# One list of items for each feed-forward, a last product by seven, and x turned in the first group

## Chip, cores and metric

The kernel runs on one core of a Trainium2 chip. The metric is the device time of one execution in microseconds (us); lower is better.

## The reference

One layer of a hybrid encoder block, 256 tokens of width 2048, fp32, with two SwiGLU feed-forwards of inner width 5632 around a mixer and a cross-attention:

```python
x = x + 0.5 * swiglu_ffn(rms_norm(x, ffn1_norm), ffn1_w_in, ffn1_w_out)   # FF1
h = rms_norm(x, mix_norm); p = h @ w_mix_in
...                                          # convolution module | spatial gating
x = x + y @ w_mix_out
x = x + memory_cross_attention(rms_norm(x, xattn_norm), rms_norm(mem, mem_norm), w_q, w_kv, w_o)
x = x + 0.5 * swiglu_ffn(rms_norm(x, ffn2_norm), ffn2_w_in, ffn2_w_out)   # FF2
return rms_norm(x, final_norm)

def swiglu_ffn(h, w_in, w_out):
    gate, up = jnp.split(h @ w_in, 2, axis=-1)
    return (jax.nn.silu(gate) * up) @ w_out
```

## The kernel before

**Products.** Each fp32 operand is split in two parts, hi (a rounding cast on ScalarE, ACT) and lo (the rest, a subtract on VectorE, DVE), and each product is three matmuls on TensorE (PE): hi·hi, hi·lo, lo·hi. A weight tile arrives as `raw` (128 partitions x 1024 columns, 512 KB, a DMA on SyncE's queue, SP), is cast and subtracted into an `hl` tile (hi and lo, 8 KB a partition), and is read by PE as the moving operand, 512 columns at a time; the activations are the stationary operand.

**Feed-forward.** The first product of each has 11 groups of 512 gate and 512 up columns, and each group has 16 k-tiles, taken as 8 pairs. `PATTERNS` says how each pair is multiplied: C is plain, 24 matmuls of 128x512; S is "by seven", with sums of blocks of weights and of activations as operands, 7 products and 21 matmuls. In the seven, DVE builds the sums of weights (L500, L501, L507, L514 of before), each of which then is cast and subtracted like a tile. The first group is plain. For the k-tiles in `SUMMED` the lo part comes from a GpSimd DMA that adds to the negated hi, not from DVE. At a group's end `give` makes silu(gate)·up (L550), transposes it on DVE (L553), and stores it to DRAM (`h_away`). The second product needs h again: `back` loads it in four DMAs of 128 KB into a tile called `z` or `h`, and `turn` splits it into hA, hB and hC, the stationary operands. Each of 11 groups has two turns.

FF1's last product runs in two blocks of 1024 columns with 44 pairs, 11 of them by seven (5 in the first block, 6 in the second). FF2's last product runs as four blocks of 512 columns, all plain (`gemm_n`, L215 to L217; the last block token half by token half, `by_token`, L1337 to L1339), with 128 small DVE transposes beside it, which turn x from its feature-major tile xT into x2, where the result is added. Behind it come the final rms, the scaling (`give` of FF2) and the output.

**Order.** Loads, casts and subtracts are each kept in the order in which they were written (`in_turn`); where these stand among other work, and where everything else stands, a scheduler decides at build time. Tiles are taken in rotation: three `hl` tiles of a pool, two in `ring`, `hl_l` twice, `hl_h`, and, in FF1, half of `more`; four `raw` tiles of a pool, `spare`'s parts and `raw_h`.

**Addresses.** Tiles have a start address within a partition. In the program built from before every tile that PE reads as a 512-wide moving operand starts at a multiple of 64 bytes, but hl_h: it starts 32 bytes past one (217056). hl_l, the tile below it, reaches to 216064 in its last 512 columns. Two pads, `to_64` and `to_64_too` (L1316), are 32 bytes each.

Of the kernel before, what the change touches and what calls it, by code (L numbers as in the profile page):

```python
# [11 lines left out]
F32 = mybir.dt.float32  # L12
# [24 lines left out]
PATTERNS = ("SCSCSCCC", "SCSCSCCC")  # L37

SUMMED = ((2, 7, 13), (2, 7, 13))
# [3 lines left out]
OUT_S = ((9, 11, 13, 15, 17), (9, 11, 13, 15, 17, 19))  # L43
OUT_STEPS = (
    [0, 1, 2, 3, 4, 5, 6, 7, 8, 10, 9, 12, 11, 14, 13, 16, 15, 18, 17, 19, 20, 21],
    [9, 0, 11, 1, 13, 2, 15, 3, 17, 4, 19, 5, 6, 7, 8, 10, 12, 14, 16, 18, 20, 21],
# [31 lines left out]
def layer(ctx: ExitStack, tc: tile.TileContext, a: dict):  # L78
# [184 lines left out]

    def square_into(acc, x, first):
# [90 lines left out]

    class FeedForward:
# [4 lines left out]


        def __init__(self, stack, tags, x_hl, gain, w_in, pattern, summed, w_out=None, pair=False):
            self.w_out, self.out_forms = w_out, None
            self.x_hl, self.gain, self.w_in, self.pattern = x_hl, gain, w_in, pattern
            self.tags, self.pattern_sums = tags, summed
            self.spairs = [p for p, c in enumerate(pattern) if c == "S"]
# [6 lines left out]
            self.places = [back[:, 0], back[:, 1], self.stage[1]]  # L374
            self.away = [dram.tile([4, 32, 4, 2 * P], F32, name=f"h_away{j}{int(pair)}") for j in range(NG)]
            self.low = ExitStack()
            low = self.low.enter_context(tc.tile_pool(name="low", bufs=1))
            more = [low.tile([P, 2, 1024], F32R, name=f"hl_l{i}") for i in range(2)]
# [3 lines left out]
            more.append(high.tile([P, 2, 1024], F32R, name="hl_h"))  # L382
            over = high.tile([P, 1024], F32, name="raw_h")
            ring = big.tile([P, 4, 2, 1024], F32R, name="ring", tag=tags[0])
            self.ring = [ring[:, i] for i in range(2)] + more
# [5 lines left out]
            self.x2 = spare[:, :4096].rearrange("p (t d) -> p t d", t=2)  # L391
            self.free = spare[:, 4096:]
            self.sums = spare[:, 4096:5120]
            self.raws = [spare[:, i * 1024:(i + 1) * 1024] for i in (5, 0, 1, 2, 3)]
            self.raw_at = 0

            self.raws_summed = [self.raws.pop()]
            self.u = [spare[:, 6144 + i * 512:6144 + (i + 1) * 512] for i in range(4)]
            self.at = 0
            self.next = self.pe = None  # L400
            self.hA = self.hB = self.hC = None
            if pair:
                self.hls.append(self.ring.pop())
                self.raws_summed.append(over)
            else:
                self.raws.append(over)

        def parts(self, raw, n=1024, last=False):

            i = self.at % (3 + len(self.ring))  # L410
            self.at += 1
            hl = whl.tile([P, 2, 1024], F32R, name="hl") if last or i < 3 else self.ring[i - 3]
            self.cast = in_turn("cast", nc.scalar.copy(out=hl[:, 0, :n], in_=raw[:, :n]))  # L413
            newest[0] = in_turn("sub", nc.vector.tensor_tensor(  # L414
                out=hl[:, 1, :n], in0=raw[:, :n], in1=hl[:, 0, :n].bitcast(F32), op=ALU.subtract
            ))
            return hl

        def raw(self, j, k):
            i = self.raw_at % (4 + len(self.raws))  # L420
            self.raw_at += 1
            raw = wraw.tile([P, 1024], F32, name="raw") if i < 4 else self.raws[i - 4]

            self.load = in_turn("load", nc.sync.dma_start(
                out=raw, in_=self.w_in[j, :, k] if j < NG else self.w_out[j - NG, :, k]
            ))
            return raw

        def buffer(self, at):
            return at % 2  # L430

        def following(self, at):
            same = [i for i in range(at + 1, len(self.sums_at)) if self.buffer(i) == self.buffer(at)]
            return same[0] if same else None

        def summed(self, at):

            if at >= len(self.sums_at):
                return
            j, k = self.sums_at[at]  # L440
            raw, hl = self.raws_summed[self.buffer(at)], self.hls[self.buffer(at)]
            nc.sync.dma_start(out=raw, in_=self.w_in[j, :, k])
            nc.scalar.activation(out=hl[:, 1], in_=raw, func=AF.Copy, scale=-1.0)
            nc.scalar.copy(out=hl[:, 0], in_=raw)
            nc.gpsimd.dma_start(out=hl[:, 1], in_=self.w_in[j, :, k], accum_op=ALU.add)

        def summed_then(self, at):

            with tc.issue_after(self.load.ins), tc.issue_after(self.cast.ins):
                self.summed(at)  # L450

        def sides(self, i):

            k = 2 * self.spairs[i]
            xg = self.u[2 * (i % 2)].rearrange("p (k t) -> p k t", k=2)
            f = self.u[2 * (i % 2) + 1].rearrange("p (f n) -> p f n", f=4)
            for q in range(2):
                nc.scalar.activation(out=xg[:, q], in_=xT[:, k + q], func=AF.Copy, scale=self.gain(k + q))
            a11, a21, a12, a22 = xg[:, 0, :P], xg[:, 0, P:], xg[:, 1, :P], xg[:, 1, P:]
            nc.vector.scalar_tensor_tensor(out=f[:, 0], in0=a21, scalar=-1.0, in1=a22, op0=ALU.mult, op1=ALU.subtract)  # L460
            nc.vector.scalar_tensor_tensor(
                out=f[:, 1], in0=f[:, 0], scalar=-1.0, in1=a11, op0=ALU.mult, op1=ALU.subtract
            )
            nc.vector.tensor_tensor(out=f[:, 2], in0=a11, in1=a21, op=ALU.subtract)
            nc.vector.tensor_tensor(out=f[:, 3], in0=a12, in1=f[:, 1], op=ALU.subtract)
            split(self.forms[i][:, :, 0], self.forms[i][:, :, 1], f)
# [9 lines left out]
        def tied(self):  # L476

            return nullcontext() if self.pe is None else tc.issue_after(self.pe.ins)

        def noted(self, done):  # L480
            if self.pe is not None:
                self.pe = done
# [942 lines left out]
```

## Time and profile before

| | |
|---|---|
| median of 3 runs | 2082.53 us (2080.94 to 2082.72) |
| profiled execution | 2083.68 us; span of its instructions 2081.9 us |
| granted TensorE clock | 0.998 of full speed |
| PE busy | 2062.0 us, 99% of the span |
| DVE busy | 1656.1 us, 80% |
| ACT busy | 1165.8 us, 56% |
| moved by DMA | 465.42 MB, 224 GB/s mean |

In the profile's rows a line number is a line of the program; `acc<-hl,x_hl` names what is written and what is read, the moving operand first. "128*128 128x512" is a stationary tile of 128x128 and a moving one of 512 columns. A matmul's row gives its time from start to end; matmuls overlap, so the interval between two starts is shorter. "[1.48 <-ACT hl_h L413]" is idle time and what ended it. `x4` stands for four instructions in one row.

### The profile page before, as it was taken

What the parts mean: (1) busy time and instruction counts of PE and PEld (TensorE: products, weight loads), DVE (VectorE), ACT (ScalarE), POOL (GpSimd) and SP (SyncE); (2) the same over time, 40 slices, a digit from 0 to 9 for tenths busy, and PEclk for the clock granted to TensorE, in tenths of its full rate; (3) what the DMA queues carried; (4) which work ended last, traced back from release to release, by engine and by line L of the source; (5) the groups of instructions that cost most, each with busy time, mean ns of one, the idle gap of its engine ahead of it and who ended that gap; (6) DMA issues with size and microseconds to landing.
All of it is one profiled execution on the core that took longest, in us unless ns stands there. A gap on an engine that the chain in (4) does not pass through costs nothing.

```text
span 2081.9 us, 26631 instructions
## 1 busy us (share of the span) xinstructions
PE 2062.0 (99%) x9577; PEld 1719.7 (83%) x9577; DVE 1656.1 (80%) x2358; ACT 1165.8 (56%) x1480; POOL 67.7 (3%) x83
## 2 busy tenths in 40 slices
PE   9999999999999999999999999999999999989998
PEld 7788888888888888888888899888888888868886
DVE  6988888878897689889877666778888888876754
ACT  7666666545555554444665455565665566544443
POOL 0000000000000000000000000000000000000000
PEclk9999999999999999999999999999999999999999
DMA  9889888868666676666656543687888888776664
GB/s 366 264 262 280 258 242 258 261 198 264 193 200 236 205 239 199 182 182 185 181 192 194 187 157 124 199 313 223 260 257 261 242 250 258 215 224 194 193 192 152
DMA packets 138372, 465.42 MB, mean 224 GB/s; under 512 B 15360, under 2 KB 27008, under 8 KB 137856
## 3 DMA queue, kind: packets, MB, share of 16 engines
q1 hardware_dynamic: 129024, 430.15, 63.1%
q0 software_dynamic: 8640, 32.51, 8.5%
q8 instruction: 75, 1.23, 0.2%
q10 hardware_dynamic: 576, 1.06, 0.1%
q14 instruction: 57, 0.47, 0.1%
HBM read 450.03 MB, written 13.63 MB: 223 GB/s over the span
## 4 chain that ended last, share of the span: by engine, by line
PE 94%; DMA 2%; DVE 2%; SPq 0%; ACT 0%; issue 0%; POOL 0%; DVEq 0%; ACTq 0%
PE acc L345 12%; PE acc L347 12%; PE acc L344 12%; PE acc L166 8%; PE acc L216 8%; PE acc L217 8%; PE acc L215 8%; PE acc L174 4%; PE acc L332 4%; PE acc L331 4%; PE acc L333 4%; PE aux L331 1%; PE aux L332 1%; PE aux L333 1%; DMA z<-h_away 1%; PE acc L1338 1%
## 5 line engine op out<-in xcount | busy, mean ns | idle before, releaser
L136 ACT CAST hl<-raw 128x1024 fp32r<-128x1024 f32 (+1 forms) x315 | 326.8, 1040 | 355.9 <-PE acc L217 189.1
L137 DVE TENSOR_TENSOR hl<-raw,hl 128x1024 fp32r<-128x1024 f32 (+1 forms) x315 | 380.7, 1210 | 160.9 <-ACT hl L136 159.1
L413 ACT CAST hl<-raw 128x1024 fp32r<-128x1024 f32 (+1 forms) x109 | 106.6, 993 | 71.3 <-DVE raw L514 44.2
L414 DVE TENSOR_TENSOR hl<-raw,hl 128x1024 fp32r<-128x1024 f32 (+1 forms) x109 | 124.7, 1151 | 18.7 <-ACT hl L413 18.3
L414 DVE TENSOR_TENSOR hl<-spare,hl 128x1024 fp32r<-128x1024 f32 (+1 forms) x94 | 106.8, 1151 | 16.0 <-ACT hl L413 15.9
L413 ACT CAST hl<-spare 128x1024 fp32r<-128x1024 f32 (+1 forms) x94 | 91.3, 993 | 48.2 <-DVE spare L514 36.0
L345 PE MATMUL acc<-hl,x_hl 128*128 128x512 f32 x304 | 111.3, 391 | 0.5 <-DVE hl L414 0.4
L344 PE MATMUL acc<-hl,x_hl 128*128 128x512 f32 x304 | 107.6, 391 | 0.0
L216 PE MATMUL acc<-hl,x_hl 128*128 128x512 f32 x256 | 100.5, 393 | 0.0
L216 PE MATMUL acc<-hl,m_hl 128*128 128x512 f32 x256 | 100.3, 392 | 0.0
L217 PE MATMUL acc<-hl,m_hl 128*128 128x512 f32 x256 | 100.2, 392 | 0.0
L217 PE MATMUL acc<-hl,x_hl 128*128 128x512 f32 x256 | 99.9, 390 | 0.0
L347 PE MATMUL acc<-hl,x_hl 128*128 128x512 f32 x304 | 94.8, 390 | 0.0
L215 PE MATMUL acc<-hl,x_hl 128*128 128x512 f32 x256 | 90.9, 393 | 0.0
L215 PE MATMUL acc<-hl,m_hl 128*128 128x512 f32 x256 | 90.9, 392 | 0.0
L413 ACT CAST hl_l<-spare 128x1024 fp32r<-128x1024 f32 (+1 forms) x60 | 58.6, 991 | 32.6 <-DVE spare L514 24.8
L414 DVE TENSOR_TENSOR hl_l<-spare,hl_l 128x1024 fp32r<-128x1024 f32 (+1 forms) x60 | 68.2, 1148 | 10.2 <-ACT hl_l L413 10.2
L413 ACT CAST ring<-spare 128x1024 fp32r<-128x1024 f32 (+1 forms) x55 | 53.2, 985 | 33.5 <-DVE spare L514 27.9
L345 PEld LDWEIGHTS acc<-hl,x_hl 128*128 128x128 f32 x304 | 57.0, 188 | 13.0 <-DVE hl L414 1.3
L593 DVE TENSOR_TENSOR spare<-spare,acc 128x512 f32<-128x512 f32 x80 | 51.0, 681 | 21.0 <-PE acc L347 20.9
L344 PEld LDWEIGHTS acc<-hl,x_hl 128*128 128x128 f32 x304 | 57.3, 189 | 12.0
L414 DVE TENSOR_TENSOR ring<-spare,ring 128x1024 fp32r<-128x1024 f32 (+1 forms) x55 | 62.3, 1140 | 6.1 <-ACT ring L413 5.8
(617 smaller groups left out, 5539.2 us busy)
## 6 DMA issues: line engine op xcount, KB each, us to landing
spare<-in_ffn_w_in SPq DMA_DIRECT2D x173, 512.0 KB, 6.9
raw<-in_ffn_w_in SPq DMA_DIRECT2D x149, 512.0 KB, 6.2
raw<-in_ffn_w_out SPq DMA_DIRECT2D x138, 512.0 KB, 4.4
raws_out<-in_ffn_w_out SPq DMA_DIRECT2D x33, 512.0 KB, 5.1
raw<-in_w_mix_vg SPq DMA_DIRECT2D x32, 512.0 KB, 4.6
raw<-in_w_k SPq DMA_DIRECT2D x32, 512.0 KB, 3.9
raw<-in_w_v SPq DMA_DIRECT2D x32, 512.0 KB, 4.4
raw<-in_w_mix_out SPq DMA_DIRECT2D x32, 512.0 KB, 4.5
```

The costliest lines, as they stand in the source:

```text
L136: nc.scalar.copy(out=hl[:, 0, :size], in_=raw[:, :size])
L137: newest[0] = nc.vector.tensor_tensor(out=hl[:, 1, :size], in0=raw[:, :size], in1=hl[:, 0, :size].bitcast(F32), op=ALU.subtract)
L166: done = nc.tensor.matmul(acc, lhsT=hi[:, k], rhs=xs[k], start=first and k == 0, stop=last and k == kk - 1, skip_group_check=True,)
L215: nc.tensor.matmul(acc[t], lhsT=x[:, 0, s], rhs=hi[:, k], start=k0 + k == 0, stop=False)
L216: nc.tensor.matmul(acc[t], lhsT=x[:, 0, s], rhs=lo[:, k], start=False, stop=False)
L217: nc.tensor.matmul(acc[t], lhsT=x[:, 1, s], rhs=hi[:, k], start=False, stop=k0 + k == nk - 1)
L331: nc.tensor.matmul(acc, lhsT=x[0], rhs=hi, start=first, stop=False)
L344: nc.tensor.matmul(acc[t][g], lhsT=x[:, 0, s], rhs=hi[:, cols[g]], start=(t, g) in first, stop=False)
L345: nc.tensor.matmul(acc[t][g], lhsT=x[:, 0, s], rhs=lo[:, cols[g]], start=False, stop=False)
L347: done = nc.tensor.matmul(acc[t][g], lhsT=x[:, 1, s], rhs=hi[:, cols[g]], start=False, stop=last)
L413: self.cast = in_turn("cast", nc.scalar.copy(out=hl[:, 0, :n], in_=raw[:, :n]))
L414: newest[0] = in_turn("sub", nc.vector.tensor_tensor(out=hl[:, 1, :n], in0=raw[:, :n], in1=hl[:, 0, :n].bitcast(F32), op=ALU.subtract))
```

## The change

1. A class `Line` runs each feed-forward as one list of items in the order of PE's products. An item has loads, a cast and a subtract (`produce`, `subtract`), the products (`use`) and further parts (`post`). The list takes places for `hl` and `raw` tiles as they come free, and at its end ties every engine's instructions in the order in which they were written. A subtract is written after the next item's cast.
2. FF2's last product takes FF1's form: two blocks of 1024 columns, 11 of 44 pairs by seven in both feed-forwards (5 and 6). Only its last four items go token half by token half.
3. FF2's x is turned in its first group: eight DVE transposes of 128x512 (`x_turn`) into the tiles h and z, two stores of 1 MB (`x_away`), and in the second block eight loads (`x_again`) and the final gains, 3 MB together. For that, the host lays out x's features in another order.
4. The turns of h stand at the last six items of group 10 (turns 0 to 5) and at the first sixteen of block 0 (6 to 21); each pair of turns issues the load of a later group's h.
5. Both feed-forwards now have the same `SUMMED` tiles, (7, 13) in group 1, and both use `more`. raw_h and the pad to_64_too are dropped.

The core of the diff:

```diff
-SUMMED = ((2, 7, 13), (2, 7, 13))
-OUT_S = ((9, 11, 13, 15, 17), (9, 11, 13, 15, 17, 19))
+SUMMED = tuple([()] + [(7, 13)] + [(2, 7, 13)] * 8 + [(2, 7)] for _ in range(2))
+OUT_S = ((9, 11, 13, 15, 17, 19), (9, 11, 13, 15, 17, 19))
...
+        def subtract(self):
+            item, self.ahead = self.ahead, None
+            if item.make is None:
+                n, hl = item.n, item.hl
+                nc.vector.tensor_tensor(
+                    out=hl[:, 1, :n], in0=item.raw[:, :n], in1=hl[:, 0, :n].bitcast(F32), op=ALU.subtract
+                )
+            for key in item.frees:
+                self.raws.append(item.held[key][1])
+            self.fetch()
...
+            for s, item in enumerate(self.items):
+                if self.ahead is item:
+                    self.subtract()
+                if item.use is not None:
+                    item.use(item.hl)
+                if item.place is not None:
+                    self.places.append(item.place)
+                self.used = s + 1
+                self.produce()
+                for part in item.post:
+                    part()
+            last = {}
+            for i in traced[begin:]:
+                if i.engine in last:
+                    tc.add_manual_dep(
                        i, last[i.engine].name,
                        mybir.DependencyInfo(mybir.DependencyClass.NoSync, mybir.DependencyReason.DATA),
                        reason="line",
                    )
+                last[i.engine] = i
...
-            high.tile([P, 248], F32, name="to_1024")
-            over = high.tile([P, 1024], F32, name="raw_h")
...
+            if j == NG - 1:
+                flat[1].post.append(lambda: (ff.back(0), ff.back(1)))
+                flat[4].post.append(lambda: ff.back(2))
+                for i, item in enumerate(flat[-6:]):
+                    item.post.insert(0, ff.turn(i))
...
-        acc_0 = gemm_n(a["ffn2_w_out"][0], h, per=0.55, between=turns, after=0)
+        parts, _, _ = ff.block(0, first_place, lambda o: None)
+        flat = [item for part in parts for item in part]
+        for i in range(6, 2 * NG):
+            flat[i - 6].post.append(ff.turn(i))
...
-        st.tile([P, 8], F32, name="to_64_too")
...
+        after = {k: [lambda k=k: x_turn(k - 1)] for k in range(1, 9)}
+        after[6].append(x_leaves(0))
+        after[10] = [x_leaves(1)]
```

Without `to_64_too` all that lies behind the pool of small tiles moves by 32 bytes. In the program built from after, the tiles `more`, `hl_s`, `hl_out`, `hl_l`, `hl_h`, `hC`, `k_hl`, `p_hl`, `q_hl`, `v_hl`, `o` and a few small ones start 32 bytes past a multiple of 64; ring, the pool's hl, x_hl and more_out stay on a multiple. Counted over the instructions, 2610 matmuls of 512 columns read a moving operand that starts so (357 before), 192 of 256 columns (none), 16 of 128 (none), and 866 a stationary one (none).

SP's queue at the start of FF1, before (`h<-in_x` and `z<-in_x` are the loads of x for the squares, `gx<-in_xT` those of the transposed x):

```order
L647 DMA raw<-in_ffn_w_in 128x512 x2
L424 DMA raw<-in_ffn_w_in 128x1024
L741 DMA gx<-in_xT 128x512
L424 DMA raw<-in_ffn_w_in 128x1024
L733 DMA h<-in_x 128x1024
L424 DMA raw<-in_ffn_w_in 128x1024
L741 DMA gx<-in_xT 128x512
L424 DMA spare<-in_ffn_w_in 128x1024
L733 DMA h<-in_x 128x1024
L424 DMA spare<-in_ffn_w_in 128x1024
```

And now:

```order
L910 DMA raw<-in_ffn_w_in 128x512 x2
L420 DMA raw<-in_ffn_w_in 128x1024
L920 DMA gx<-in_xT 128x512
L889 DMA h<-in_x 128x1024
L420 DMA raw<-in_ffn_w_in 128x1024 x2
L920 DMA gx<-in_xT 128x512
L889 DMA h<-in_x 128x1024
L420 DMA spare<-in_ffn_w_in 128x1024 x2
L920 DMA gx<-in_xT 128x512
```

The first load of x stood behind weight tiles 1 and 2 (tile 0 is the one in halves) and now stands behind tile 1 alone; the others have moved up in the same way.

DVE's queue at the end of FF1's first group, before (L550 is the gating, L553 the transpose, L414 a subtract, L500 to L514 the sums of weights for a seven):

```order
L414 TENSOR_TENSOR hl_l_134<-spare,hl_l_134 128x1024
L414 TENSOR_TENSOR hl_h<-spare,hl_h 128x1024
L500 TENSOR_TENSOR spare<-raw 128x512
L501 TENSOR_TENSOR spare<-raw 128x512
L507 TENSOR_TENSOR raw<-spare,raw 128x512
L550 SCALAR_TENSOR_TENSOR h<-acc,r_x_111,h 128x4x128 x2
L553 STREAM_TRANSPOSE h<-h 128x1024
L414 TENSOR_TENSOR hl_h<-spare,hl_h 128x1024
L414 TENSOR_TENSOR more<-raw,more 128x1024
L414 TENSOR_TENSOR hl<-raw,hl 128x1024
L500 TENSOR_TENSOR spare<-raw 128x512
L501 TENSOR_TENSOR spare<-spare,raw 128x512
```

And now (L714 the gating, L717 the transpose, L428 a subtract, L628 to L635 the sums; `hl_l_134` and `hl_l_135` are the two tiles hl_l):

```order
L632 TENSOR_TENSOR raw<-sums,raw 128x512
L428 TENSOR_TENSOR hl<-sums,hl 128x1024
L428 TENSOR_TENSOR hl<-raw,hl 128x1024
L635 TENSOR_TENSOR raw<-raw 128x512
L428 TENSOR_TENSOR hl<-raw,hl 128x1024
L428 TENSOR_TENSOR ring<-raw,ring 128x512
L428 TENSOR_TENSOR ring<-raw,ring 128x1024
L628 TENSOR_TENSOR sums<-spare 128x512
L629 TENSOR_TENSOR sums<-spare 128x512
L428 TENSOR_TENSOR hl_l_134<-raw,hl_l_134 128x1024
L714 SCALAR_TENSOR_TENSOR h<-acc,r_x_111,h 128x4x128 x2
L717 STREAM_TRANSPOSE h<-h 128x1024
```

The subtracts of the first pair by seven and of the plain pair behind it have moved ahead of the gating and the transpose.

SP's queue at the entry of FF2's last product, before (`h_away` numbers go by group, 11122 is group 2):

```order
L560 DMA h<-h_away_11122 32x4x256 x4
L133 DMA raw<-in_ffn_w_out 128x1024
L560 DMA z<-h_away_11123 32x4x256 x4
L560 DMA z<-h_away_11124 32x4x256 x4
L560 DMA h<-h_away_11125 32x4x256 x4
L560 DMA z<-h_away_11126 32x4x256 x2
L133 DMA raw<-in_ffn_w_out 128x1024
L560 DMA z<-h_away_11126 32x4x256 x2
L133 DMA raw<-in_ffn_w_out 128x1024
L560 DMA z<-h_away_11127 32x4x256 x3
L133 DMA raw<-in_ffn_w_out 128x1024
L560 DMA z<-h_away_11127 32x4x256
```

And now (`b_` numbers go by group, 11112 is group 0; the rows begin in group 10):

```order
L420 DMA raw<-in_ffn_w_in 128x1024 x4
L726 DMA z<-b_11112 32x4x256 x4
L726 DMA z<-b_11113 32x4x256 x4
L720 DMA b_11121<-h 128x1024
L726 DMA h<-b_11114 32x4x256 x4
L420 DMA raw<-in_ffn_w_out 128x1024 x4
L726 DMA z<-b_11115 32x4x256 x4
L420 DMA raws_out<-in_ffn_w_out 128x1024 x4
L420 DMA raw<-in_ffn_w_out 128x1024 x2
L726 DMA z<-b_11116 32x4x256 x4
L420 DMA raw<-in_ffn_w_out 128x1024
L726 DMA h<-b_11117 32x4x256 x4
```

h's first loads have moved ahead of the second product's first weights, of which now ten tiles are issued before the load of group 4's h.

More of the change, by code (lines that the diff above doesn't have):

```diff
@@ L400, in __init__ @@
-            self.next = self.pe = None
+            self.raws_summed = [raws.pop() for _ in range(2)]
+            self.sums_at = [(j, k) for j in range(1, NG) for k in sums[j]]
             self.hA = self.hB = self.hC = None
[L402 to L434, printed above, removed]
@@ L447, in summed_then @@
[L447 to L462, printed above, removed]
[L463 to L466 removed]
+            self.out_forms = None
@@ new lines, in banks, with begins, into @@
+        def banks(self, b, names):
+            for name in names:
+                b[name] = bank(pa if name in "67" else ps, "aux" if name in "67" else "acc")
+        def begins(self, b, name):
+            first = name not in b["begun"]
+            b["begun"].add(name)
+            return first
+        def into(self, b, name, x, hi, lo, last=False):
+            if name not in b:
+                self.banks(b, "5761" if name in "5761" else "2348")
+            three(b[name], x, hi, lo, self.begins(b, name), last)
@@ new lines, in second_sum, with third_sum, use, go @@
+            def second_sum():
+                nc.vector.tensor_tensor(out=one()[:, lo], in0=sums[:, lo], in1=two()[:, hi], op=ALU.add)
+            def third_sum():
+                nc.vector.tensor_tensor(out=one()[:, lo], in0=two()[:, lo], in1=one()[:, lo], op=ALU.subtract)
+            def use(*parts):
+                def go(w):
+                    for name, x, s in parts:
+                        self.into(b, name, x(), w[:, 0, s], w[:, 1, s], last and name in "5761")
+                return go
@@ new lines, in x_again, with next_turn @@
+        def x_again():
+            nonlocal xT
+            line.raws.extend(ff.fixed([ff.sums]))
+            xT = xt.tile([P, KD, T], F32, name="xT", tag="x")
+            for k in range(0, KD, 8):
+                nc.gpsimd.dma_start(out=xT[:, k:k + 8], in_=a["xT"][:, k:k + 8])
+            rest["x_hl"] = gained_tile("S2")
+        def next_turn():
+            rest["turns"].pop(0)()
+        last = items[ff.ends[NG - 1] - 1]
+        items[ff.ends[NG - 1] - 5].post.append(raws_out)
+        last.post.append(more_out)
@@ L847, in layer @@
+        line.run()
+        turns = turned(rest["o2"], 1)
         x_hl = rest["x_hl"]
-        finish()
         r_mt = rms_cols(sm, D, "r_mt")
@@ new lines, in layer, with quarters @@
+        after[9] = [x_sums]
+        items = ff.begin(
+            lambda k: None, after, (r_x, inverse_root_parts(r_x, lambda: x_tot[0][:, 0, 0:2], 1.0 / D, RMS_EPS))
+        )
+        items[14].post.append(lambda: given(ff))
+        groups(ff, items)
+        rest = {}
+        sums = st.tile([P, 2, 4], F32, name="sums")
+        most = [st.tile([P, 1], F32, name=f"f_most{t}") for t in range(2)]
+        def quarters(o):
+            return [o[:, t, g * G:(g + 1) * G] for g in range(2) for t in range(2)]
@@ L1354, in layer @@
-        give(1, 4)
+        items[ff.ends[NG - 1] - 5].post.append(raws_out)
+        items[ff.ends[NG - 1] - 1].post.append(more_out)
+        parts, _, _ = ff.block(0, first_place, lambda o: None)
+        flat = [item for part in parts for item in part]
+        for i in range(6, 2 * NG):
+            flat[i - 6].post.append(ff.turn(i))
+        flat[16].post.append(hl_out)
+        items += flat
+        ff.in_high[0].until = len(items) - 1
+        parts, b, _ = ff.block(1, second_place, None)
```

910 lines of the change are left out of this document (555 added, 355 removed).

## The prediction

> **What bounds the kernel now.** I read the page first (span, busy shares, clock), then the groups of TensorE (PE) by form, then PE's waits, then windows and timelines around the few places where PE stands still.
>
> ```profile
> span 2081.9 us, 26631 instructions
> PE 2062.0 (99%) x9577; PEld 1719.7 (83%) x9577; DVE 1656.1 (80%) x2358; ACT 1165.8 (56%) x1480; POOL 67.7 (3%) x83
> PEclk9999999999999999999999999999999999999999
> L215 PE MATMUL acc<-hl,hB 128*128 128x512 f32 x96 | 33.5, 389 | 0.0
> ```
>
> PE is busy for 99% of the span at full clock, so the time is the number of matmuls times their interval, plus the few stalls. The 389 ns of the last row is one matmul from start to end; they overlap. The interval has to be read from starts:
>
> ```profile
> 22.86 1.07 PE L344 MATMUL acc<-hl_l,x_hl 128*128 128x512 f32 x4
> ...
> 25.58 1.10 PE L344 MATMUL acc<-hl_h,x_hl 128*128 128x512 f32 x4
> ...
> 28.38 1.09 PE L344 MATMUL acc<-hl,x_hl 128*128 128x512 f32 x4
> ...
> 31.12 1.07 PE L344 MATMUL acc<-hl,x_hl 128*128 128x512 f32 x4
> L345 PE MATMUL acc<-ring,x_hl 128*128 128x512 f32 x168 | 62.5, 389 | 0.0
> L345 PE MATMUL acc<-hl_l,x_hl 128*128 128x512 f32 x156 | 58.6, 389 | 0.0
> L345 PE MATMUL acc<-hl_h,x_hl 128*128 128x512 f32 x96 | 37.1, 396 | 0.0
> L347 PE MATMUL acc<-hl_h,x_hl 128*128 128x512 f32 x96 | 31.0, 396 | 0.0
> ```
>
> These are four k-tiles of one plain item, twelve 128x512 matmuls each. Twelve on hl_l take 25.58 − 22.86 = 2.72 us, 226.7 ns each; twelve on hl_h take 28.38 − 25.58 = 2.80 us, 233.3 ns each. So hl_h costs 6.7 ns more for each matmul, and the groups say the same of the whole kernel: 396 ns against 389 wherever hl_h is the moving operand. hl_h is in before the only moving tile of this width that starts 32 bytes past a multiple of 64 (front part: addresses). 6.7 of 226.7 ns is 3.0%, as one 64-byte piece more would be on the 32 pieces of a 2048-byte row; that reading is mine, the 6.7 ns is the trace's.
>
> The stalls stand in PE's waits and in three windows (busy us, instruction count):
>
> ```profile
> PE acc L216 <- DVE hl L137: 3.4, 3, 2.1
> PE acc L215 <- ACT hl L136: 3.0, 1, 3.0
> PE acc L331 <- ACT hl_h L413: 1.5, 1, 1.5
> 45.00:60.00 15.00, 13.10 (x53) 9.18 (x52) 9.44 (x12) 6.03 (x8) 0.00 (x0) 1.00 0.81 276
> 450.00:490.00 40.00, 39.15 (x169) 31.07 (x168) 38.16 (x59) 27.99 (x40) 0.00 (x0) 1.00 0.91 273
> 1828.00:1864.00 36.00, 29.56 (x119) 22.96 (x118) 28.23 (x46) 16.35 (x22) 0.00 (x0) 0.95 0.70 219
> ```
>
> The second and third columns are the window and PE's busy time with its matmuls. At 226.7 ns each, the loss is 15.0 − 53 × 0.2267 = 3.0 us at the end of the first group of FF1, 40.0 − 169 × 0.2267 = 1.7 us at the entry of FF1's last product, and 36.0 − 119 × 0.2267 = 9.0 us at the entry of FF2's last product. The chain of waits says what that last one is:
>
> ```profile
> 1811.40 3.93 DMA z<-h_away
> 1815.41 6.14 DMA raw<-in_ffn_w_out
> 1821.58 7.04 DMA z<-h_away
> 1832.89 2.43 DMA z<-h_away
> 1848.37 5.35 DMA raw<-in_ffn_w_out
> ```
>
> h comes back from DRAM and the new weights come in on one SP queue, each held up by the other's buffers, with PE waiting for the split weights at the end.
>
> **The change, part by part.** The sum is against the profiled execution (2083.68 us; the median of the runs is 1.15 us below, and I subtract that at the end).
>
> *Eleven pairs by seven in FF2's last product.* By the order of both kernels PE issues 8394 matmuls of 128x512 instead of 8427: 11 pairs × 3 = 33 fewer, 33 × 0.2267 = −7.5 us, all on the path. The additions it needs (five of 128x512 a pair on DVE, one more subtract) are paid beside PE, as FF1's last product does already.
>
> *Entry of FF2's last product.* Now the first two turns' loads stand ahead of the last weights of group 10, six turns fall inside group 10, and ten weight tiles are ahead of the next wait for h (third order fence). I take the 9.0 us as gone: −9.0. If the queue holds up in another way, up to all of it stays; that is a rival.
>
> *End of the first group of FF1.* What PE waits for there is DVE:
>
> ```profile
> 50.00 0.75 DVE L550 SCALAR_TENSOR_TENSOR h<-acc,r_x,h 128x512 f32<-128x512 f32 x1 [6.86 <-ACT h L548]
> 51.72 1.25 DVE L553 STREAM_TRANSPOSE h<-h 128x1024 f32<-128x1024 f32 x1
> 52.89 1.18 DVE L414 TENSOR_TENSOR hl_h<-spare,hl_h 128x1024 fp32r<-128x1024 f32 x1
> 53.99 1.21 DVE L414 TENSOR_TENSOR more<-raw,more 128x1024 fp32r<-128x1024 f32 x1
> ```
>
> DVE idles 6.86 us, then does the gating and the transpose, and only then the subtracts of the first pair by seven. The new order puts the six subtracts of the first pair by seven and of the plain pair after it ahead of the gating (second order fence): they fall into the idle time. −3.0 us. Next late would be the second pair's first subtract, behind gating and transpose (2 × 0.75 + 1.25 = 2.75 us), while PE has 21 + 24 matmuls (10.2 us) ahead of it: covered.
>
> *Entry of FF1's last product.* −1.7 us by the same reasoning as FF2's; 0 is the other end. The same window shows how little room there is: DVE is busy 38.16 of 40 us. In both last products the turns go on over block 0's first sixteen items, one an item, so DVE keeps that density, now in a pinned order in which a late instruction delays all behind it. No row shows that order; with 5% of some 45 us of slack in each product, I bound it by 0 and 5 us for both and take +1.0, nearer to 0, because FF1's 1.7 us came with a worse order.
>
> *Start of FF1.* The loads of x for the squares now stand ahead of weight tiles 2, 4, 6 and 8 on SP (first order fence), and each subtract stands behind the next tile's x_hl on DVE.
>
> ```profile
> GB/s 0 0 0 51 66 309 391 399 395 436 385 332 369 373 336 377 336 303 336 369 410 344 315 279 377 389 434 418 451 401 385 430 393 451 407 391 429 416 406 430
> 7.03 1.03 ACT L413 CAST hl<-raw 128x1024 fp32r<-128x1024 f32 x1
> 8.20 1.22 DVE L414 TENSOR_TENSOR hl<-raw,hl 128x1024 fp32r<-128x1024 f32 x1
> ```
>
> At 390 GB/s (the first slices of the first 20 us) 512 KB take 1.34 us, and here PE runs as fast as weights arrive. One load ahead of tile 2 makes it 1.34 us late; later ones displace nothing that x loads did not displace before. +1.4 us with the subtract, between 0 and 3.
>
> *x turned in FF2's first group.* 128 small transposes beside the last product go; eight of 128x512 come, on DVE, which leads PE by several tiles there; two stores of 1 MB and 3 MB of later loads go on SP, the latter at 390 GB/s 8 us, with eight weight tiles (eight times 2.72 us of PE work) ahead of them. Nothing on the path: 0. If that cover fails, 1 to 3 us.
>
> *Tail.* After the last matmul:
>
> ```profile
> 2071.57 1.29 POOL L1283 TENSOR_TENSOR spare<-spare,gf 128x512 f32<-128x512 f32 x1 [53.71 <-ACT sq L1282]
> 2072.56 0.39 PE L1339 MATMUL acc<-hl,hC 128*128 128x512 f32 x1
> 2073.33 0.68 DVE L1278 SCALAR_TENSOR_TENSOR spare<-acc,spare 128x512 f32<-128x512 f32 x1
> ```
>
> The last add begins 0.4 us after PE's last end. Afterwards token half 0's scaling and two blocks are queued ahead of it: +0.4, between 0 and 2 (one POOL multiply more, 1.29, and one add, 0.68).
>
> *Where the tiles start.* The change drops a pad of 32 bytes, and the tiles behind it (more, hl_s, hl_out, hl_l, hl_h, hC) now start 32 bytes past a multiple of 64. By the order and addresses 2610 of the 512-wide matmuls read such a moving tile, against 357. If what slows hl_h is its start, 2253 × 6.7 ns = +15.1 us; 192 matmuls of 256 (k_hl, p_hl) at the same step +1.3. hC, hl_s, q_hl, v_hl and others are stationary: 866 loads. One takes 188 ns:
>
> ```profile
> L345 PEld LDWEIGHTS acc<-hl,x_hl 128*128 128x128 f32 x304 | 57.0, 188 | 13.0 <-DVE hl L414 1.3
> ```
>
> That hides under 226.7 ns with a step of 6.7 ns added, so I take 0; if it didn't hide, 866 × 6.7 = 5.8 us. The Trainium skill, SBUF — State Buffer, section "Operand start alignment", asks of an operand only that it start at a multiple of its element size, and adds that "these runs timed nothing". By that rule alone the start would cost nothing and the sum would be 16.4 us lower; the rows of hl_h disagree with it as a rule of speed.
>
> **Sum.** −7.5 − 9.0 − 3.0 − 1.7 + 1.0 + 1.4 + 0.4 + 15.1 + 1.3 = −2.0 us: 2081.7 profiled, 2080.5 as a median (−0.1%). A difference under 0.2%, 4.2 us, is about what a measurement here can't tell from none.
>
> **Rivals.**
> - *The start costs nothing* (hl_h is slow for its place at the top of the memory, where no other moving tile lies in before). For it: the one tile has both properties. Against it: hl_l reaches within 1 KB of it at 389 ns, and the 3.0% fits one piece in 32. Then only the 201 additional matmuls on hl_h cost, 1.3 us instead of 16.4: 2080.5 − 15.1 = 2065.4.
> - *FF2's entry stalls as before* (the one that ends slower). Place: SP, where the loads of h for turns 8 on wait for turn 3's buffers while weights wait behind them. For it: the same queue carried 3.93, 6.14 and 7.04 us pieces of the chain. Against: ten weight tiles, 27 us of PE work, stand ahead. If the first blocked load outlasts these, the 9.0 us stay: 2089.5. It decides once more than 6 us of them stay.
> - *The starts slow weight loads too*: +5.8, 2086.3.
> - *A wait over 3 us comes anew.* In before the matmuls after the 3.04 us wait ran at half speed for some time:
>
> ```profile
> 1857.19 0.62 PE L216 MATMUL acc<-hl,hA 128*128 128x512 f32 x1
> 1857.61 0.63 PE L217 MATMUL acc<-hl,hA 128*128 128x512 f32 x1
> ```
>
> An interval of 0.42 us instead of 0.227, from 1857.2 to 1860.6: eight matmuls, 1.6 us more. It is within the ranges above, not a case of its own.
>
> **How the numbers follow.** The sum as it stands 0.68 (its own range 2076 to 2086, from −4.5 with the bounds of start, tail and entries at their good ends to +5.5); start free 0.12; entry stalls 0.10; weight loads 0.10. The first case gives faster in a third of it (0.22), same in nearly all the rest; start free is faster; the entry is slower; weight loads are half same, half slower; the first case's upper end adds 0.03 to slower. Together faster 0.35, same 0.47, slower 0.18, the open terms tilting a little to faster. The range 2065 to 2088 leaves out about half of the start-free case and most of the entry's.
>
> **What would show it.** Matmuls on more, hl_s, hl_l and hl_out at 396 ns instead of 389; no wait on PE near 50 us; none over 1 us in the last products; 8394 matmuls of 128x512. If hl_l stays at 389, the term of 15.1 is wrong; if PE waits for hl in FF2's last product, the entry is; if the first twelve us lose more than 3, the start is.

## The result, and the profile after

Over 20 runs the changed kernel takes 2085.74 us (median; 2083.71 to 2092.58), against 2081.62 us before (median of 18): ratio 1.002, 95% interval 1.0013 to 1.0028. Runs far longer than the rest are left out of all medians here: two of before above, and one each in e4, e5, e11 and before's first series. It is slower by 0.2%, where 0.1% faster was forecast. The profiled execution took 2084.38 us, so it lies 1.4 us under its median, while that of before (2083.68) lies 2.1 us over. A second profile of the changed kernel (e8 below, 2087.41 us) lies on the other side; both are used.

The page after:

```profile
span 2082.6 us, 26581 instructions
PE 2068.9 (99%) x9544; PEld 1713.2 (82%) x9544; DVE 1703.4 (82%) x2358; ACT 1197.7 (58%) x1514; POOL 62.8 (3%) x81
```

33 matmuls fewer, and yet PE is busy for 6.9 us more. The groups by form say where:

```profile
L359 PE MATMUL acc<-ring,x_hl 128*128 128x512 f32 x152 | 59.2, 390 | 0.0
L359 PE MATMUL acc<-hl_l,x_hl 128*128 128x512 f32 x168 | 66.5, 396 | 0.0
L359 PE MATMUL acc<-more,x_hl 128*128 128x512 f32 x168 | 66.5, 396 | 0.0
L358 PE MATMUL acc<-hl_h,x_hl 128*128 128x512 f32 x80 | 31.6, 396 | 0.0
L361 PE MATMUL acc<-hl,hA 128*128 128x512 f32 x136 | 41.9, 389 | 0.0
L361 PE MATMUL acc<-hl,hC 128*128 128x512 f32 x60 | 18.9, 395 | 0.0
```

Every tile that moved by 32 bytes and is read 512 columns wide as a moving operand now takes what hl_h took, beside a stationary tile that did not move (hl_s and hl_out, not shown, too: 395 to 397 ns). In the last two rows the moving tile hl starts where it did, and only the stationary tile differs: hC, which moved, costs 6 ns more than hA, which did not.

Windows of after, at the start, at the ends of the first two groups, and at the entries of both last products:

```profile
0.00:20.00 20.00, 16.32 (x69) 13.72 (x70) 8.73 (x13) 11.53 (x18) 0.70 (x6) 1.00 0.92 340
45.00:60.00 15.00, 14.64 (x64) 11.56 (x63) 13.84 (x20) 11.04 (x13) 1.02 (x1) 1.00 0.76 269
85.00:105.00 20.00, 19.89 (x87) 15.93 (x86) 18.82 (x25) 9.43 (x11) 0.88 (x1) 1.00 0.78 253
450.00:490.00 40.00, 40.00 (x175) 32.59 (x174) 28.84 (x34) 20.91 (x27) 0.00 (x0) 1.00 0.76 244
1828.00:1864.00 36.00, 36.00 (x159) 29.40 (x158) 31.88 (x50) 22.94 (x34) 0.00 (x0) 1.00 1.00 278
1864.00:1900.00 36.00, 36.00 (x159) 29.55 (x158) 32.25 (x51) 21.78 (x30) 0.00 (x0) 1.00 0.89 259
```

And the second profile (e8), behind the entry of FF2's last product, which starts at 1850.2 us there:

```profile
1864.00:1900.00 36.00, 35.20 (x152) 28.01 (x151) 29.76 (x51) 20.08 (x30) 0.00 (x0) 1.00 0.92 229
```

In the first profile both entries are full. FF2's last product starts at 1829.6 us in before and at 1848.8 us in after, so its entry lies in the last two rows: 159 matmuls in each 36 us, where before has 119. FF1's starts at 483.2 us in before and at 487.8 us in after: 175 matmuls in the 40 us where there were 169, and 176 in the 40 us behind them. DVE's load there has moved more than it has shrunk: 28.84 of the first 40 us where there were 38.16, and 36.04 of the next 40 where there were 29.89. The end of the first group holds 64 matmuls instead of 53. The start is worse: 69 matmuls in the first 20 us. Before has these rows there and at the end of the second group:

```profile
0.00:20.00 20.00, 18.94 (x82) 16.51 (x83) 13.16 (x25) 16.67 (x30) 0.70 (x6) 1.00 0.92 338
85.00:105.00 20.00, 20.00 (x89) 16.50 (x88) 18.85 (x25) 9.16 (x12) 0.87 (x1) 1.00 0.77 241
```

### The profile page after: what moved, and what is told of

It reads as the page before. It is cut to its first block, busy times and chain, and to the rows that moved or that the text cites. A ratio compares the mean times of both kernels' runs of the same rounds, so it can differ in the third digit from the quotient of the medians.

```text
span 2082.6 us, 26581 instructions
## 1 busy us (share of the span) xinstructions
PE 2068.9 (99%) x9544; PEld 1713.2 (82%) x9544; DVE 1703.4 (82%) x2358; ACT 1197.7 (58%) x1514; POOL 62.8 (3%) x81
## 4 chain that ended last, share of the span: by engine, by line
PE 93%; DVE 2%; DMA 1%; ACT 1%; issue 0%; POOL 0%; DVEq 0%; ACTq 0%; SPq 0%
PE acc L359 15%; PE acc L358 15%; PE acc L361 15%; PE acc L158 8%; PE acc L208 5%; PE acc L209 5%; PE acc L207 5%; PE acc L345 5%; PE acc L346 5%; PE acc L347 5%; PE acc L166 4%; PE aux L345 2%; PE aux L346 2%; PE aux L347 2%; DMA raw<-in_memT 1%; DVE hl L129 0%
## 5 line engine op out<-in xcount | busy, mean ns | idle before, releaser
L128 ACT CAST hl<-raw 128x1024 fp32r<-128x1024 f32 (+1 forms) x228 | 235.6, 1035 | 224.6 <-PE acc L209 92.8
L129 DVE TENSOR_TENSOR hl<-raw,hl 128x1024 fp32r<-128x1024 f32 (+1 forms) x228 | 273.9, 1203 | 95.6 <-ACT hl L128 94.5
L451 ACT CAST hl<-raw 128x1024 fp32r<-128x1024 f32 (+1 forms) x136 | 134.3, 1000 | 94.6 <-PE acc L361 38.1
L428 DVE TENSOR_TENSOR hl<-raw,hl 128x1024 fp32r<-128x1024 f32 (+1 forms) x136 | 156.6, 1156 | 26.8 <-ACT hl L451 25.1
L208 PE MATMUL acc<-hl,x_hl 128*128 128x512 f32 x256 | 100.7, 393 | 0.2 <-DVE hl L129 0.2
L209 PE MATMUL acc<-hl,x_hl 128*128 128x512 f32 x256 | 99.9, 390 | 0.0
L359 PE MATMUL acc<-hl,x_hl 128*128 128x512 f32 x248 | 97.0, 391 | 2.6 <-DVE hl L428 2.6
L358 PE MATMUL acc<-hl,x_hl 128*128 128x512 f32 x248 | 97.1, 392 | 0.0
L207 PE MATMUL acc<-hl,x_hl 128*128 128x512 f32 x256 | 90.3, 392 | 0.0
L361 PE MATMUL acc<-hl,x_hl 128*128 128x512 f32 x248 | 76.4, 389 | 0.0
L451 ACT CAST hl<-raws_out 128x1024 fp32r<-128x1024 f32 (+1 forms) x53 | 51.0, 968 | 43.9 <-PE acc L361 22.3
L451 ACT CAST hl<-spare 128x1024 fp32r<-128x1024 f32 (+1 forms) x52 | 49.4, 968 | 34.9 <-DVE spare L635 18.0
L428 DVE TENSOR_TENSOR hl<-raws_out,hl 128x1024 fp32r<-128x1024 f32 (+1 forms) x53 | 59.1, 1121 | 10.5 <-ACT hl L451 9.3
L428 DVE TENSOR_TENSOR hl<-spare,hl 128x1024 fp32r<-128x1024 f32 (+1 forms) x52 | 57.4, 1116 | 12.1 <-ACT hl L451 11.4
L451 ACT CAST hl<-sums 128x1024 fp32r<-128x1024 f32 x34 | 35.7, 1049 | 54.4 <-DVE sums L629 53.8
L359 PE MATMUL acc<-hl_l,x_hl 128*128 128x512 f32 x168 | 66.5, 396 | 0.0
L359 PE MATMUL acc<-more,x_hl 128*128 128x512 f32 x168 | 66.5, 396 | 0.0
L358 PE MATMUL acc<-more,x_hl 128*128 128x512 f32 x168 | 66.5, 396 | 0.0
L358 PE MATMUL acc<-hl_l,x_hl 128*128 128x512 f32 x168 | 66.4, 395 | 0.0
```

Source lines behind the costliest of these rows:

```text
L128: nc.scalar.copy(out=hl[:, 0, :size], in_=raw[:, :size])
L129: newest[0] = nc.vector.tensor_tensor(out=hl[:, 1, :size], in0=raw[:, :size], in1=hl[:, 0, :size].bitcast(F32), op=ALU.subtract)
L207: nc.tensor.matmul(acc[t], lhsT=x[:, 0, s], rhs=hi[:, k], start=k0 + k == 0, stop=False)
L208: nc.tensor.matmul(acc[t], lhsT=x[:, 0, s], rhs=lo[:, k], start=False, stop=False)
L209: nc.tensor.matmul(acc[t], lhsT=x[:, 1, s], rhs=hi[:, k], start=False, stop=k0 + k == nk - 1)
L358: nc.tensor.matmul(acc[t][g], lhsT=x[:, 0, s], rhs=hi[:, cols[g]], start=(t, g) in first, stop=False)
```

## The experiments

Times are medians; before, run beside them on the same chip, had 2082.2 us in the first series (e1 to e4), 2083.1 us in the second (e5 to e8) and 2082.6 us in the third (e9 to e12). Ratios are to before; a difference between two series is uncertain by about the 0.9 us between these. Each cut of code is against the kernel that the run builds on, and "..." stands for lines left out.

### e1_pad: the pads put back

```diff
     st.tile([P, 8], F32, name="to_64")
+    st.tile([P, 8], F32, name="to_64_too")
...
             highs = [high.tile([P, 2, 1024], F32R, name="hl_h")]
+            high.tile([P, 8], F32, name="to_64_high")
```

> The changed kernel with two pads of 32 bytes put in, one in the pool of small tiles and one behind hl_h, so that every 512-wide moving operand and every stationary one of the products starts at a multiple of 64 bytes; the order of instructions on all engines is that of the changed kernel. Theory (the start sets the interval): 2610 moving tiles of 512 and 192 of 256, and some 500 stationary ones that stand beside an aligned moving tile, lose 6.7 ns each: 22 us less, near 2064 us, all groups at 389 ns. Rival (the start costs nothing, something else in the new order makes these matmuls slower, such as DMA or DVE traffic to the same tiles): 2084 to 2087 us, hl_l and more still at 396 ns.

2071.02 us, ratio 0.9942 (0.9928 to 0.9956): 14.7 us under the changed kernel, with the same order of instructions. Where the tiles start thus costs most of what was forecast, but hl_h, now on a multiple of 64, stayed slow:

```profile
L360 PE MATMUL acc<-hl_l,x_hl 128*128 128x512 f32 x168 | 65.4, 389 | 0.0
L360 PE MATMUL acc<-more,x_hl 128*128 128x512 f32 x168 | 65.5, 390 | 0.0
L360 PE MATMUL acc<-hl_h,x_hl 128*128 128x512 f32 x80 | 31.5, 394 | 0.0
```

So 22 us was too much by hl_h's 558 × 6.7 ns = 3.7 us, by the 256-wide matmuls, which cost nothing (below), and by a wait of 2 us that this profile shows at 98 us.

### e2_before_hl_h: hl_h alone, in the kernel before

```diff
-            high.tile([P, 248], F32, name="to_1024")
+            high.tile([P, 240], F32, name="to_1024")
...
             over = high.tile([P, 1024], F32, name="raw_h")
+            high.tile([P, 8], F32, name="to_64_high")
```

> The kernel before with hl_h moved down by 32 bytes, to a multiple of 64, and nothing else; it stays at the top of the memory. Theory (the start): its 357 matmuls go from 396 to 389 ns, 357 x 6.7 ns = 2.4 us less. Rival (the place at the top of the memory): hl_h stays at 396 ns and the time within 0.5 us.

2082.84 us, ratio 1.0001 (0.9992 to 1.001), hl_h at 394 ns:

```profile
L345 PE MATMUL acc<-hl_h,x_hl 128*128 128x512 f32 x96 | 36.9, 394 | 0.0
```

The theory of the prediction, "past a multiple of 64", fails here, and the rival (the place) would hold if this run stood alone.

### e3_before_mis: the kernel before without its pad

```diff
-        st.tile([P, 8], F32, name="to_64_too")
```

> The kernel before without its pad of 32 bytes: more, hl_s, hl_out, hl_l, hC and some others start 32 bytes past a multiple of 64; the order is that of before. Theory (the start of moving operands): 2019 instead of 357 moving tiles of 512 and 193 of 256, (1662 + 193) x 6.7 ns = 12.4 us more; if stationary tiles cost as much, up to 881 x 6.7 = 5.9 us on top, 18 at most. Rival (start free): no change.

2098.93 us, ratio 1.0074 (1.0061 to 1.0087), 16.7 us more, with the order of before unchanged. So 32 bytes alone move the time by as much as the theory said, and stationary tiles cost too. Counted with the intervals under e5, the tiles give 13.5 of the 16.7 us; the rest is not placed. The group of L217 with hC, in before:

```profile
L217 PE MATMUL acc<-hl,hC 128*128 128x512 f32 x48 | 18.7, 389 | 0.0
```

and without the pad:

```profile
L217 PE MATMUL acc<-hl,hC 128*128 128x512 f32 x48 | 19.0, 396 | 0.0
```

### e4_start: the first 20 us mended

```diff
+                if self.ahead is not None and item.at < KD:
+                    self.subtract()
                 if item.pre is not None:
                     item.pre()
...
-            if k in (2, 4, 6, 8):
-                beside_load.append(x_load(k // 2 - 1))
+            if k in (3, 5, 10, 13):
+                beside_load.append(x_load((3, 5, 10, 13).index(k)))
```

> As the changed kernel with the two pads, and FF1's first group mended: the loads of x stand behind weight tiles 2, 4, 9 and 12 as in before, and each subtract of the first group ahead of the next tile's x_hl. Theory (the 2.9 us that PE loses more in the first 20 us come from these two): 3 us less than with the pads alone. Rival (they come from transfers of the start that are late anyway): within 1 us of it.

2067.44 us, ratio 0.9924 (0.991 to 0.9938), 3.6 us under e1. PE's two waits for a subtract in the first 15 us are gone; the changed kernel has them in this row:

```profile
PE acc L359 <- DVE hl L428: 2.6, 2, 1.4
```

The run undoes the order of the loads and that of the subtracts together, so what each of them costs is not separated. What is left of PE's waits stands at the ends of the first two groups, and there it has grown: e1 waits 0.6 us at the first and 1.9 us at the second, e4 1.9 and 2.9 us:

```profile
PE acc L346 <- DVE spare L706: 2.9, 1, 2.9
PE acc L346 <- ACT h L716: 1.9, 1, 1.9
```

### e5_probe: the step of the start

```diff
+            self.own.tile([P, 16], F32, name="by_64")
             self.hls = [self.own.tile([P, 2, 1024], F32R, name="hl_s")]
...
+            for i, n in enumerate((16, 32)):
+                low.tile([P, n], F32, name=f"by_low{i}")
+                lows.append(low.tile([P, 2, 1024], F32R, name=f"hl_l{i}"))
...
-            high.tile([P, 8], F32, name="to_64_high")
+            high.tile([P, 24], F32, name="to_128_high")
```

> As the kernel with pads and mended start (e4_start), with the tiles put at chosen distances from a multiple of 512 bytes: hl_s and hl_out 64, the first hl_l 128, the second 256, hl_h 384 (a multiple of 128, still at the top of the memory), hC 64 (stationary); all others 0. hl_h stayed slow at a multiple of 64 that is 64 past a multiple of 128, so either the place at the top counts or the step is coarser than 64. Theory (the step is 128 bytes): hl_h and both hl_l at 227 ns an interval, hl_s, hl_out and matmuls with hC at 233. Rival (place): hl_h at 233, all others at 227. Rival (the step is 512): all of them at 233. By the first the time is 336 + 300 + 354 matmuls x 6.7 ns = 6.6 us more and 558 x 6.7 = 3.7 us less than e4_start's 2067.8: about 2070.

2077.36 us, ratio 0.9976 (0.9967 to 0.9986): 9.9 us over e4. The step of 128 falls (128 and 384 bytes are slow), and so does the place as the only cause (tiles far from the top are slow too); a step of 512 is nearest, though not with 233 ns for all. Some 1400 more moving tiles than in e4 and some 540 stationary ones stand off a multiple of 512; by the intervals below they make up 7.1 of the 9.9 us, and the rest is not placed. For each 128x512 matmul I took the interval to the next start from the trace, and both operands' start addresses from the program. Mean intervals by bytes past a multiple of 512, each from the run in the last column:

| moving | stationary | interval, ns | matmuls | run |
|---|---|---|---|---|
| 0 | 0 | 227.0 | 8225 | e6 |
| 64 | 0 | 230.4 | 579 | e5 |
| 128 | 0 | 232.4 | 396 | e5 |
| 256 | 0 | 229.0 | 378 | e5 |
| 384 | 0 | 232.4 | 510 | e5 |
| 448 | 0 | 233.3 | 558 | e1 |
| 480 | 0 | 233.4 | 2505 | after |
| 0 | 64 | 233.2 | 440 | e5 |
| 0 | 480 | 233.3 | 440 | after |
| 480 | 480 | 229.7 | 101 | after |
| 64 | 64 | 230.6 | 53 | e5 |
| 384 | 64 | 228.9 | 48 | e5 |

What all fast tiles of before share is a start on a multiple of 512, not of 64. None of the six starts tried between two multiples is free: the cost runs from 2 to 6.4 ns for moving tiles, and is 6.2 and 6.3 ns for the two starts of stationary ones. Each start in e5 stands for one or two tiles, so tile and start are not told apart within that run. Where both operands are off the cost is not the sum: 480 with 480 and 384 with 64 take less than either alone, and 64 with 64 takes what the moving tile alone does. The 256-wide matmuls on k_hl with q_hl, both off by 480, take 120.1 ns against 119.8: nothing. One rule for the whole table I have not found; that stays open.

### e6_best: every tile on a multiple of 512

```diff
-            high.tile([P, 8], F32, name="to_64_high")
+            high.tile([P, 120], F32, name="to_512_high")
```

> As e4_start with hl_h at a multiple of 512 bytes, so that every tile of the products starts at one. Theory (the start alone counts): hl_h's 558 matmuls lose 6.7 ns each, 3.7 us less than e4_start's 2067.8: 2064. Rival (place): 2068 and hl_h still at 396 ns.

2063.56 us, ratio 0.9909 (0.9895 to 0.9924), 3.9 us under e4, and the place falls: hl_h is where it was, at the top of the memory, and runs like the others.

```profile
L359 PE MATMUL acc<-hl_h,x_hl 128*128 128x512 f32 x80 | 31.1, 389 | 0.0
```

A step coarser than 512 is not seen: the moving tiles of this run stand 512, 1024 or 1536 bytes past a multiple of 2048 and take 226.7, 226.7 and 227.1 ns.

### e7_sumload: SP not held by the loads for the summed tiles

```diff
-            self.summed_load(at + 2)
+            self.line.due.append((self.line.used + 4, lambda: self.summed_load(at + 2)))
```

> As e6_best, with each load for a tile whose lo part GpSimd adds issued four items later on SP; nothing else moves. In the changed kernel that load stands directly behind the copies that free its buffer, and SP holds the weight loads behind it until ACT has done these. Theory (this is what PE loses at the end of the first two groups, 0.3 to 3 us each, and what makes the time vary from run to run): 2 to 4 us less than e6_best and a narrower spread. Rival (the transfers of the first 100 us are late whatever the order): within 1 us of e6_best, same spread.

2062.15 us, ratio 0.9904 (0.9888 to 0.9921), the fastest of all and 1.4 us under e6, runs between 2061.71 and 2062.87 (e6 2061.57 to 2064.20). That SP stood behind such a load is seen in e4 (SP's queue: the store of h, the summed tile's load, weights):

```profile
65.53 0.43 SPq L724 DMA_DIRECT2D a<-h  x1
69.81 0.33 SPq L563 DMA_DIRECT2D spare<-in_ffn_w_in  x1
71.06 0.33 SPq L421 DMA_DIRECT2D spare<-in_ffn_w_in  x1
71.43 3.71 SPq L421 DMA_DIRECT2D raw<-in_ffn_w_in  x4
```

Five weight loads go out behind it, in one burst. But 1.4 us are no more than four runs of each can tell apart, and e7's own profile loses 4.8 us at the end of group 0. Whether the load's place matters is not settled.

### e8_after_again: the changed kernel, a second profile

> The changed kernel as it is, for a second profile: its runs lie between 2083.7 and 2092.6 us and the first profiled one near the low end. Theory: PE's intervals are the same in both, and what differs is the wait at the end of the first two groups (0.5 and 0.3 us in the first profile), by as much as the two spans differ. Rival: the difference is spread over the whole run, or stands in the last products.

Span 2085.6 us, 3.0 us longer than the first profile. PE waits 2.1 us at 98 us for a sum that empties an accumulator (L702), where the first profile lost 0.3, and 0.6 and 0.2 us in FF2's last product; the start is 0.5 us better.

```profile
PE acc L345 <- DVE spare L702: 2.1, 1, 2.1
PE acc L359 <- DVE more_out L428: 0.6, 1, 0.6
PE acc L346 <- DVE hl_out L428: 0.2, 1, 0.2
```

With 152 instead of 159 matmuls in the 36 us of the window shown above, FF2's entry lost 1.6 us. Those two places make up the 3 us: the theory was half right, the rival half.

### e9_give: the gating ahead of the casts

```diff
+                if s == KD - 1:
+                    for part in item.post:
+                        part()
                 self.produce()
...
```

> As e7_sumload, with the end of each first group in another order: the gating of group 0 (two silu on ACT, two products and the transpose on DVE) and the two copies for hl_s stand ahead of the last two casts and the sums of the second pair by seven, instead of behind them. In e6_best and e7_sumload PE waits 2.4 and 2.9 us there for a silu that frees an accumulator (4.3 and 4.8 us lost in all between 50 and 60 us). Theory (the silu is late because of the casts ahead of it): 2.5 to 4 us less than e7_sumload, 2058 to 2060. Rival (the weights of that time are late, and PE then waits for a cast): within 1 us of e7_sumload.

2064.55 us, ratio 0.9912 (0.9897 to 0.9927): not faster than e7. What PE waited for in e6, on PE and then on ACT (L716 the silu, L454 the casts):

```profile
55.24 0.55 PE L346 MATMUL acc<-hl,x_hl 128*128 128x512 f32 x1 [2.37 <-ACT h L716]
...
53.55 1.04 ACT L454 CAST hl_l<-sums 128x1024 fp32r<-128x1024 f32 x1 [1.62 <-DVE sums L633]
54.51 1.26 ACT L716 ACTIVATE h<-acc,r_x 128x512 f32<-128x512 f32 x2
```

That wait went, as the theory says: the loss between 50 and 60 us falls from 4.8 (e7) to 1.1 us. Not all of the 4.8 us is the wait of 2.9 us itself: behind it eight matmuls start some 0.43 us apart, about 1.6 us more, and the granted clock is 0.89 in e7's window (first row), where it is 1.00 in e9's. The same stretch follows the wait of 2.4 us in e6; none follows e4's wait of 2.9 us at the second group's end. And a loss came back 40 us later, at the end of group 1; the last two rows are e9's windows:

```profile
45.00:60.00 15.00, 12.11 (x47) 9.57 (x46) 13.82 (x19) 11.07 (x14) 1.02 (x1) 0.89 0.78 261
45.00:60.00 15.00, 14.22 (x64) 11.43 (x63) 13.92 (x18) 11.48 (x14) 1.02 (x1) 1.00 0.78 242
85.00:105.00 20.00, 18.00 (x80) 14.64 (x79) 18.89 (x25) 10.50 (x13) 0.88 (x1) 1.00 0.76 245
```

Its runs spread from 2060.7 to 2066.5, and the profiled one is the lowest. Counted at 227 ns each, the matmuls that start in the first 110 us leave 5.4 us of them in before, 6.7 and 8.1 in the two profiles of after, 7.4 in e1, 6.7 in e4, 6.0 in e7 and 4.2 in e9: a good part of what is mended at one place returns at the next.

### e10_late_back: h asked for late in FF2

```diff
-                flat[1].post.append(lambda: (ff.back(0), ff.back(1)))
-                flat[4].post.append(lambda: ff.back(2))
+                late = ff.tags[0] == "S0"
+                flat[-7 if late else 1].post.append(lambda: (ff.back(0), ff.back(1)))
+                flat[-6 if late else 4].post.append(lambda: ff.back(2))
```

> As e7_sumload, but in FF2 the loads of h for the first three groups of turns are issued one item ahead of the first turn (behind the last weights of group 10) instead of at the second and fifth item of group 10. This takes away one part of the change, the early start of h. Theory (in before PE lost 9 us at this place because the loads of h and of weights waited for each other): the turns come 4 to 7 us late, the pinned order holds the subtracts behind them, and PE loses 3 to 9 us more than in e7_sumload near 1830 to 1880. Rival (the five tiles of lead hide it): within 1 us.

2065.95 us, ratio 0.9921 (0.9906 to 0.9936), 3.8 us more than e7, with a wait of 2.0 us (2.4 us lost) on PE at 1822 us that e7 does not have:

```profile
PE acc L359 <- DVE spare L709: 2.0, 1, 2.0
```

The first turns' subtracts run up to 7 us later than in e7 (from 1812.6 instead of 1805.4 us), and the sums that PE waits for (L709) stand behind them on DVE. The theory holds at its lower end: the early loads are a part of what took the 9 us away, not all of it.

### e11_unpinned: the same program without the ties

```diff
-            last = {}
-            for i in traced[begin:]:
-                if i.engine in last:
-                    tc.add_manual_dep(
...
-                last[i.engine] = i
```

> As e7_sumload without the ties that keep every engine's instructions within a feed-forward in the order in which they were written; the scheduler places them again. Theory (the written order is worth something): the entries of the last products and the first groups show waits again, 2 to 8 us more than e7_sumload. Rival (the order hardly matters once tiles and places are the same): within 1 us.

2084.14 us, ratio 1.0012 (0.9999 to 1.0024), 22.0 us more than e7: both theories fell, the first by being far too small. The waits are spread over the whole run (its profiled run was one of the fastest, at 2079.35); the longest:

```profile
PE acc L360 <- DVE more_out L430: 2.6, 2, 1.4
PE aux L346 <- DVE spare L695: 2.4, 1, 2.4
PE acc L346 <- DVE spare L696: 1.3, 1, 1.3
```

The written order is thus worth more than the 33 matmuls. It is not the better one everywhere: at the ends of the first two groups this profile has no wait, and from 45 to 60 us it holds 67 matmuls, where e7 has 47 and e9 64.

### e12_fewer: 5 instead of 11 pairs by seven in FF2's last product

```diff
-    for _ in range(2)
+    for _ in range(1)
 )
+OUT_STEPS += ((([0, 1, 2, 3, 4, 5, 6, 7, 8, 10, 9, 12, 11, 13, 14, 15, 16, 17, 18, 19, 20, 21], (9, 11)),
+               ([9, 0, 11, 1, 13, 2, 3, 15, 4, 17, 5, 19, 6, 7, 8, 10, 12, 14, 16, 18, 20, 21], (9, 11, 13))),)
```

> As e7_sumload with 5 instead of 11 pairs of FF2's last product by seven; the sums of activations are still made for all 11. Theory (PE alone bounds it): 18 matmuls of 128x512 more, 18 x 0.2267 = 4.1 us more. Rival (DVE's sums and subtracts for a pair by seven cost PE something there): less than 4.1 us more.

2067.04 us, ratio 0.9928 (0.9911 to 0.9944), 4.9 us more than e7 for 18 matmuls (4.1 us): within the spread, each matmul saved is worth its interval.

## Why the prediction was wrong, step by step

The sum was −2.0 us; the spans of the two profiles stand at +0.7 and +3.7 us, and the medians at +4.1. By its terms, in us (losses of windows at 226.7 ns a matmul, as in the prediction):

| term | predicted | first profile of after | how |
|---|---|---|---|
| 33 fewer matmuls | −7.5 | −7.5 | e12: 18 gave 4.9 |
| entry of FF2's last product | −9.0 | −9.0 | 159 matmuls in 36 us, twice |
| end of FF1's first group | −3.0 | −2.5 | 64 matmuls in 15 us |
| end of the second group | none | +0.3 (second +2.3) | e8's wait |
| entry of FF1's last product | −1.7 | −1.7 | 175 in 40 us |
| end of FF1's last product, 645 us | none | −1.0 | two waits of before, 0.36 and 0.27 us, gone with what follows them |
| turns in a pinned order | +1.0 | 0 (second +1.6) | 152 instead of 159 in 36 us |
| start of FF1 | +1.4 | +2.9 | 69 instead of 82 matmuls in 20 us |
| tail | +0.4 | +0.6 | last add 0.94 us after PE's end, 0.38 before |
| moving tiles off | +16.4 | +14.7 | (2505 − 354) × 6.7 ns, 101 × 2.7 |
| stationary tiles off | 0 | +2.9 | 440 × 6.6 ns |
| rest | 0 | +1 | what is left of +0.7; in the mixer (660 to 1380 us) PE's time over the intervals under e5 is 5.4 us in before and 6.3 in after |

Right: the matmuls, the three stalls, the direction and most of the size of the start addresses. With every tile on a multiple of 512, and the start mended, the change gives what its other parts promise: e6 lies 0.9% under before. One reading was off without harm: the 1.7 us called the entry of FF1's last product stand just ahead of it, at 455, 461 and 480 us, while the product's first matmul starts at 483.2 us.

The steps that failed:

1. *"That hides under 226.7 ns with a step of 6.7 ns added, so I take 0."* It doesn't hide. A stationary tile 32 bytes past a multiple of 64 (480 past one of 512) lengthens the interval as much as a moving one (rows of hC above; 233.3 ns). The weight load itself is recorded no longer on the moved hC (187 and 188 ns in after) than on hA (188 ns), so a load that stays shorter than the interval is no cover; the case was a rival at one in ten. It cost 2.9 us. The moving tiles came 1.7 us under their term, so that the two together missed by 1.2.
2. *The start, +1.4.* It lost 2.9 us, in two waits of 1.2 and 1.4 us for a subtract and what follows them. Both times the subtract stands on DVE right behind the next tile's x_hl; the first time it starts at 9.33 us, though its cast on ACT ended at 7.6 us, and the second time the weight tile was late as well (its cast began at 11.84 us). I had added nearly nothing for the subtract.
3. *The pinned order's bound was put on the wrong place.* I searched in the last products; it was the end of the second group, which the prediction doesn't name. There PE lost 0.3 and 2.3 us in the two profiles. Without the ties there is no wait there (e11), which speaks for the order as the cause, but no run of the changed kernel itself takes the ties away. The rival "entry stalls as before" did not occur, though 1.6 us of it showed once.
4. *The unit.* "32 bytes past a multiple of 64" gave the right count here, since every tile that the change moved also left a multiple of 512; as a rule it is wrong (e2), and so was the reading of one piece in 32.

That the first profile comes within 2.7 us of the sum is in part luck: the turns that cost nothing, the 1.0 us at 645 us and the moving tiles' 1.7 us made up for much of what was missed.

The Trainium skill, SBUF — State Buffer, "Operand start alignment", is about legality, as it says itself; e3 shows what it leaves out, 16.7 us for 32 bytes.

## What to carry to other kernels

When a kernel is bound by TensorE, put every tile that its matmuls read, moving or stationary, on a multiple of 512 bytes (shown here for fp32 operands 512 columns wide; 256 columns with both tiles off showed no cost), and look at the groups by form for one tile name that is some ns slower than the others: a pad that looks idle was worth 16.7 us, and one of 480 bytes 4. A sum of many small parts must name each wait's successor: of a start mended by 3.4 us (15 matmuls more in e4's first 20 us than in after's) some 2 us came back at the ends of the next groups, and so did 2 us of a gating moved by 3.7 us (e9). An order that is written out and tied is worth measuring by itself; here taking only the ties away cost 22.0 us.

## What the hardware showed that I had not expected

At 480 bytes off, stationary and moving operands have the same price for their start (233.3 and 233.4 against 227.0 ns), and together they take 229.7 ns, less than either alone; at 64 bytes the stationary one costs more (233.2 against 230.4 ns). DVE and ACT don't show it: in before, where hl_h is off, a cast into it takes 1045 ns and one into the pool's hl 1048, and the subtracts take the same too (the groups of DVE by form):

```profile
L414 DVE TENSOR_TENSOR hl<-spare,hl 128x1024 fp32r<-128x1024 f32 x82 | 98.6, 1218 | 9.9 <-ACT hl L413 9.8
...
L414 DVE TENSOR_TENSOR hl_h<-spare,hl_h 128x1024 fp32r<-128x1024 f32 x13 | 15.8, 1215 | 0.5 <-ACT hl_h L413 0.5
```
